# The second projection's buffers opened one tile sooner, and the last group's fourth product with its sums and splits pinned together, in an encoder layer on one core

## The chip, the core and the metric

The kernel runs on one core of a Trainium2 chip. The metric is the device time of one execution in microseconds (us). The unchanged kernel took 1143.36 us as the median of three runs (1142.58, 1143.36 and 1144.24).

## What is computed

One layer of an encoder over 1024 positions of width 1024: a norm, an input projection that feeds a pooling mixer and a chunked attention, an output projection, then a gated MLP, a per-layer gate and a last norm. The change touches only the MLP, here cut to its core:

```python
hn = rmsnorm(h, norm_ffn_g[i])
up = hn @ w_up[i]                                  # 1024 x 5632
gt, val = up[..., :D_FF], up[..., D_FF:]           # D_FF = 2816
gt = causal_dwconv(gt, conv_w[i], conv_b[i])
h = h + (jax.nn.gelu(gt, approximate=False) * val) @ w_down[i]
```

## The kernel before, in words

Every matrix product is float32. An operand is held as two parts, hi (the value rounded to the matmul type) and lo (the rest). Making the pair is a **split** (`split`, lines 132 to 137): ACT writes hi (L133), then DVE writes lo (L134). Where the operand is taken negative, the pair is L988 on ACT and L989 on DVE. `mm3` (lines 126 to 130) then issues three matmuls: hi by hi (L128), hi by lo (L129), lo by hi (L130).

The MLP's hidden width is cut into 22 tiles of 128 (`fi` from 0 to 21). For each, `up(fi, ...)` makes the gate and value rows of the tile. It uses a seven-product scheme for a two-by-two block product, so `steps` lists seven products, from `fi` = 2 on in the order 1, 5, 6, 2, 7, 3, 4. One product is 12 matmuls of 128x512. Their weights come from four quarters of `w_up`, loaded by SP into a ring of six raw buffers (`fetch`, L699). DVE adds quarters to each other where a product needs a sum (`summed`, L703), and the result is split into a ring of three (`prepare`). A raw buffer is loaded again once its last reader is done. The tile's activation is then formed on ACT and DVE: L811 and L812, the convolution L837 to L839, GELU L840, and L854/L856, or L847 in the last two tiles. For the first 20 tiles SP stores it to a scratch tensor `Yd` in DRAM (L898).

The **second projection** (by `w_down`) takes the 20 stored tiles in five groups of four (g from 0 to 4), again with seven products each, in the order 1, 2, 5, 4, 6, 7, 3. One is 24 matmuls (`down_next`), whose four results DVE adds into the residual (L1006). Both sides of a product (w: `w_down`; a: `Yd`) are loaded into the raw buffers `RW`, kinds "one" and "grow". The first source of a buffer is loaded by SP (L956) and further ones are added in flight by a DMA from POOL's queue (L954). `split_next` splits them into one set of pairs (`BQ` and a piece of `R`), so the splits for the next product must wait until PE has read the set for the last one. `ask` issues the loads whose buffers are free. In group 4, product 4, the a side is the sum of its "one" and "grow" buffers, added on DVE (L984, one for each of two buffers).

PE's order is written out by hand. The down products stand between up products: in the last two tiles, product (4, 5) follows product 3 of tile 20, and product (4, 4) follows product 1 of tile 21. The orders on DVE, ACT, SP and POOL are set when the program is built, by a scheduler that puts each instruction where its own model finds it ready. An instruction marked `keep_in_program_order` keeps its written place among the pinned ones, and `issue_after` keeps a load behind the one named. Each of these engines works strictly in its order.

`RW` and `BQ` are opened after tile 1 (L1018), in memory that an earlier buffer held, and the first loads stand behind tile 1's store. After tile 21 the tail begins, for which `late_pairs` loads and splits twelve pieces (two of `pT`, four of `w_ple`, four of `w_down`, two of `pT`; L1066) into raw buffers that the last `w_up` quarters leave.

Of the kernel before, what the change touches and what calls it, by code (L numbers as in the profile page):

```python
# [93 lines left out]
def trunk(tc, xT, pT, vecs, w_qk0, w_in, w_v, bias, counts, pool_w, w_out, w_up, w_down,  # L94
# [4 lines left out]
    with tc.tile_pool(name="sb", bufs=1) as sb, \  # L99
# [587 lines left out]
        prepared, fetched, done = [0], [0], [0]  # L687
        held = {}
        used = [False] * len(rawu)

        def fetch(upto):

            while fetched[0] < len(loads) and loads[fetched[0]][0] < upto and not used[fetched[0] % len(rawu)]:
                _, owner, (v, z) = loads[fetched[0]]
                i = fetched[0] % len(rawu)
                fetched[0] += 1
                used[i] = True
                fi = owner if isinstance(owner, int) else owner[0]
                sp.dma_start(rawu[i], w_up[fi, v, :, z * 512:(z + 1) * 512])  # L699
                held[owner, (v, z)] = i  # L700

        def summed(to, a, b, op=ALU.add):
            dve.tensor_tensor(rawu[to], rawu[a], rawu[b], op)  # L703

        def prepare(upto):
            while prepared[0] < min(upto, len(order)):
# [5 lines left out]
                if (fi, n) in alone:  # L712
                    t, = done_with = [held[(fi, n), q] for q in FORMS[n]]
                else:
                    a11, a12, a21, a22 = [held.get((fi, q)) for q in ((0, 0), (0, 1), (1, 0), (1, 1))]
                    if n == 5:
                        summed(a21, a21, a22)
                    elif n == 6:
                        summed(a21, a21, a11)
                    elif n == 3 and fi < 2:  # L720
                        summed(a11, a21, a12)
                    elif n == 7:
                        if fi > 1:
# [247 lines left out]
        def split_next(pinned=False):  # L971
# [3 lines left out]
            if not all((side, g, n) in asked for side in "wa"):  # L975
                return
            nsplit[0] += 1
            for side in "wa":
                sign = -1.0 if side == "a" and n in NEGATIVE else 1.0
                for j in range(2):  # L980
                    t = raws[side, buffer(side, n), j]
                    hi, lo = pairs[side, j]
                    if (side, g, n) == ("a", 4, 4):
                        tc.keep_in_program_order(dve.tensor_tensor(t, t, raws["a", "grow", j], ALU.add))  # L984
                    if sign > 0:
                        split(t, hi, lo, pinned)
                    else:
                        act.activation(hi, t, AF.Copy, scale=-1.0)  # L988
                        dve.scalar_tensor_tensor(lo, t, -1.0, rv(hi), ALU.mult, ALU.subtract)  # L989
                split_done.add((side, g, n))  # L990
            ask()

# [22 lines left out]

        for fi in range(4):
            up(fi, negative(fi))
            if fi == 1:  # L1018
                b_pool = tc.tile_pool(name="bq", bufs=1)
                bp = b_pool.__enter__()  # L1020
                B = bp.tile([P, 3072], F32R, name="BQ")
# [2 lines left out]
                for s, side in enumerate("wa"):  # L1024
                    for j in range(2):
                        p_ = spots[2 * s + j]
                        pairs[side, j] = p_[:, 0:512], p_[:, 512:1024]
                        for q, kind in enumerate(("one", "grow")):
                            z = 4 * s + 2 * q + j
                            raws[side, kind, j] = RW[:, 512 * z:512 * (z + 1)]  # L1030
                with tc.issue_after(written[0].ins):
                    ask()
            if fi == 2:
                for d in range(4):
# [26 lines left out]
        def late_pairs(n):  # L1061
            for _ in range(n):
                src, hi, lo = pieces[npiece[0]]
                t = late[npiece[0]]
                npiece[0] += 1
                sp.dma_start(t, src)  # L1066
                split(t, hi, lo, True)

        up(last_f[0], None, downs(last_f[0], (3, 5)))
# [217 lines left out]
```

## Time and profile before

| | |
|---|---|
| median of three runs | 1143.36 us |
| the profiled execution's own time | 1145.58 us |
| its span, first to last instruction | 1143.8 us |
| PE busy | 1129.3 us, 99% of the span |
| DVE busy | 890.4 us, 78% |
| ACT busy | 604.6 us, 53% |
| mean granted TensorE clock | 0.995 |

The profiled execution took 1.8 us more than its span, for what lies before the first and behind the last instruction. A matmul of 128x512 is shown as 0.39 us but they start about 0.227 us apart, since each overlaps the next. So a loss on PE is best seen where two starts lie further apart than that. In a row of the timeline, the bracket tells how long the engine was idle ahead of the instruction and what ended that. Several like instructions that follow each other share one row with their count.

### The profile page before, as it was taken

The numbers are of one execution on the slowest core, as the hardware profiler recorded it, in microseconds if no ns is written. First come the engines' busy times: TensorE is split into PE (matmuls) and PEld (weight loads), VectorE is DVE, ScalarE is ACT, GpSimd is POOL, SyncE is SP. The second block draws the span as 40 slices with busy tenths as digits, with TensorE's granted clock in tenths as the row PEclk, the third lists the DMA queues.
The fourth block names the chain that finished last, engine by engine and source line by source line (L and its number), as shares of the span: only waits on it lengthen the run. The fifth ranks groups of instructions, "written<-read, shape, count | busy, mean of one in ns | idle before, by whom it ended". The sixth has DMA issues, their size and how long they took to land.

```text
span 1143.8 us, 15743 instructions
## 1 busy us (share of the span) xinstructions
PE 1129.3 (99%) x5675; PEld 957.4 (84%) x5675; DVE 890.4 (78%) x1546; ACT 604.6 (53%) x1071; POOL 143.1 (13%) x188
## 2 busy tenths in 40 slices
PE   8999999999999999999999999999999999999997
PEld 7988998888888887888888888888888887888897
DVE  7678878879658887887788778877887787986864
ACT  8568677765645544434353435343534444564644
POOL 0000000073002200120112011201120112000000
PEclk9999999999999999999999999999999998999999
DMA  7110102114500146574557455745584556420012
GB/s 265 38 49 31 49 13 68 40 28 143 180 19 10 38 132 171 145 172 135 156 148 173 132 157 148 175 130 157 143 176 132 148 146 128 132 93 19 1 75 74
DMA packets 64446, 124.84 MB, mean 109 GB/s; under 512 B 7280, under 2 KB 8560, under 8 KB 64368
## 3 DMA queue, kind: packets, MB, share of 16 engines
q1 hardware_dynamic: 50400, 98.60, 26.0%
q0 software_dynamic: 13824, 25.17, 13.6%
q8 instruction: 44, 0.72, 0.3%
q14 instruction: 34, 0.28, 0.1%
q10 hardware_dynamic: 144, 0.07, 0.0%
HBM read 109.13 MB, written 14.68 MB: 108 GB/s over the span
## 4 chain that ended last, share of the span: by engine, by line
PE 87%; DVE 6%; issue 2%; ACT 2%; DMA 2%; POOL 1%; SPq 0%; DVEq 0%; POOLq 0%; ACTq 0%
PE PS L129 26%; PE PS L128 26%; PE PS L130 26%; PE PS L370 2%; DVE R L134 2%; PE PS L388 1%; PE PS L387 1%; PE PS L345 1%; PE PS L344 1%; DMA F<-in_w_up 1%; ACT R L133 1%; DMA F<-in_w_qk 1%; PE PS L353 0%; PE PS L352 0%; DVE F L703 0%
## 5 line engine op out<-in xcount | busy, mean ns | idle before, releaser
L128 PE MATMUL PS<-R 128*128 128x512 f32 (+1 forms) x1176 | 442.9, 377 | 2.7 <-ACT R L232 1.4
L130 PE MATMUL PS<-R 128*128 128x512 f32 (+1 forms) x1176 | 438.1, 373 | 0.0
L129 PE MATMUL PS<-R 128*128 128x512 f32 (+1 forms) x1112 | 420.1, 378 | 0.3 <-DVE R L233 0.3
L128 PEld LDWEIGHTS PS<-R 128*128 128x128 f32 x1176 | 221.7, 189 | 40.8 <-ACT R L232 1.8
L130 PEld LDWEIGHTS PS<-R 128*128 128x128 f32 x1176 | 221.5, 188 | 39.2 <-DVE R L134 0.4
L129 PEld LDWEIGHTS PS<-R 128*128 128x128 f32 x1112 | 209.7, 189 | 36.6 <-DVE R L233 0.6
L133 ACT ACTIVATE R<-F 128x512 fp32r<-128x512 f32 (+2 forms) x225 | 140.7, 637 | 178.7 <-PE PS L129 80.8
L134 DVE TENSOR_TENSOR R<-F,R 128x512 fp32r<-128x512 f32 (+2 forms) x221 | 152.7, 700 | 55.2 <-ACT R L133 54.3
L133 ACT ACTIVATE BQ<-RW 128x512 fp32r<-128x512 f32 x90 | 52.6, 622 | 88.6 <-PE PS L129 87.1
L1006 DVE TENSOR_TENSOR F<-F,PS 128x512 f32<-128x512 f32 x140 | 92.3, 682 | 7.4 <-PE PS L130 7.4
L703 DVE TENSOR_TENSOR F<-F 128x512 f32<-128x512 f32 x88 | 60.6, 688 | 41.0 <-DMA F<-in_w_up 39.2
L954 POOL DMA_DIRECT2D RW<-Yd x56 | 48.7, 870 | 241.1 <-DMA RW<-Yd 176.6
L954 POOL DMA_DIRECT2D RW<-in_w_down x40 | 35.7, 956 | 254.9 <-DMA RW<-in_w_down 223.0
L134 DVE TENSOR_TENSOR BQ<-RW,BQ 128x512 fp32r<-128x512 f32 x90 | 59.1, 686 | 2.5 <-PE PS L129 1.3
L128 PE MATMUL PS<-R,BQ 128*128 128x512 f32 x140 | 55.3, 395 | 1.1 <-ACT R L988 1.1
L129 PE MATMUL PS<-BQ 128*128 128x512 f32 x140 | 55.1, 394 | 0.6 <-DVE BQ L989 0.6
L356 ACT ACTIVATE F<-F,small 128x640 f32<-128x640 f32 (+2 forms) x64 | 44.4, 693 | 21.2 <-DVE small L354 13.1
L128 PE MATMUL PS<-BQ 128*128 128x512 f32 x140 | 55.1, 394 | 0.4 <-ACT BQ L988 0.4
L129 PE MATMUL PS<-R,BQ 128*128 128x512 f32 x140 | 55.2, 394 | 0.3 <-DVE R L989 0.3
L130 PE MATMUL PS<-R,BQ 128*128 128x512 f32 x140 | 55.0, 393 | 0.0
L130 PE MATMUL PS<-BQ 128*128 128x512 f32 x140 | 55.0, 393 | 0.0
L612 ACT ACTIVATE F<-F 128x512 f32<-128x512 f32 (+1 forms) x49 | 27.9, 570 | 45.5 <-DVE F L1154 16.7
(188 smaller groups left out, 1808.5 us busy)
## 6 DMA issues: line engine op xcount, KB each, us to landing
F<-in_w_up SPq DMA_DIRECT2D x91, 256.0 KB, 4.4
RW<-Yd SPq DMA_DIRECT2D x60, 256.0 KB, 3.7
RW<-Yd POOLq DMA_DIRECT2D x56, 256.0 KB, 4.9
RW<-in_w_down SPq DMA_DIRECT2D x50, 256.0 KB, 2.8
Yd<-F SPq DMA_DIRECT2D x40, 256.0 KB, 3.0
RW<-in_w_down POOLq DMA_DIRECT2D x40, 256.0 KB, 6.4
F<-in_w_in SPq DMA_DIRECT2D x10, 512.0 KB, 3.8
F<-in_xT SPq DMA_DIRECT2D x16, 256.0 KB, 5.8
```

The lines of the kernel that those rows point to most:

```text
L128: pe.matmul(ps, ahi, bhi, start=first, stop=False, skip_group_check=more)
L129: pe.matmul(ps, ahi, blo, start=False, stop=False, skip_group_check=more)
L130: pe.matmul(ps, alo, bhi, start=False, stop=last, skip_group_check=more)
L133: both = (act.activation(hi, src, AF.Copy), dve.tensor_tensor(lo, src, rv(hi), ALU.subtract))
L134: dve.tensor_tensor(lo, src, rv(hi), ALU.subtract))
L344: pe.matmul(PS[:, 4 + z, 0:320], q, K2[:, ks], start=True, stop=False)
L356: act.activation(S[:, 0:n], S[:, 0:n], AF.Exp, bias=s_[:, 0:1], scale=-1.0, accum_out=s_[:, 1:2])
L370: pe.transpose(pst[:, j * P:(j + 1) * P], S[:, j * P:(j + 1) * P], ident)
L612: act.activation(self.q, src, AF.Square)
L703: dve.tensor_tensor(rawu[to], rawu[a], rawu[b], op)
L954: pool.dma_start(t, src, accum_op=ALU.add)
L1006: dve.tensor_tensor(t, t, PS[:, 4 + d], ALU.subtract if n in (1, 5) else ALU.add)
```

## The change

Four things change. First, `RW` and `BQ` are opened after tile 0 and not after tile 1, and the first loads are held behind the latest `w_up` load instead of behind tile 1's store. Second, in the last tile the sum for product 5 (L703 with n = 5) is pinned. Third, for group 4's product 4, the two sums L984 come ahead of all its splits, and sums and splits are pinned. Fourth, the loads of `late_pairs` are held behind the latest `w_up` load.

```diff
@@ fetch
-                sp.dma_start(rawu[i], w_up[fi, v, :, z * 512:(z + 1) * 512])
+                newest[0] = sp.dma_start(rawu[i], w_up[fi, v, :, z * 512:(z + 1) * 512])
@@ prepare
                     if n == 5:
-                        summed(a21, a21, a22)
+                        s5 = summed(a21, a21, a22)
+                        if fi == NF - 1:
+                            tc.keep_in_program_order(s5)
@@ split_next
             nsplit[0] += 1
+            if (g, n) == (4, 4):
+                pinned = True
+                for j in range(2):
+                    t = raws["a", "one", j]
+                    tc.keep_in_program_order(dve.tensor_tensor(t, t, raws["a", "grow", j], ALU.add))
             for side in "wa":
                 sign = -1.0 if side == "a" and n in NEGATIVE else 1.0
                 for j in range(2):
                     t = raws[side, buffer(side, n), j]
                     hi, lo = pairs[side, j]
-                    if (side, g, n) == ("a", 4, 4):
-                        tc.keep_in_program_order(dve.tensor_tensor(t, t, raws["a", "grow", j], ALU.add))
                     if sign > 0:
                         split(t, hi, lo, pinned)
                     else:
                         act.activation(hi, t, AF.Copy, scale=-1.0)
-                        dve.scalar_tensor_tensor(lo, t, -1.0, rv(hi), ALU.mult, ALU.subtract)
+                        low = dve.scalar_tensor_tensor(lo, t, -1.0, rv(hi), ALU.mult, ALU.subtract)
+                        if pinned:
+                            tc.keep_in_program_order(low)
@@ the loop over the first four tiles
             up(fi, negative(fi))
-            if fi == 1:
+            if fi == 0:
                 b_pool = tc.tile_pool(name="bq", bufs=1)
...
-                with tc.issue_after(written[0].ins):
+                with tc.issue_after(newest[0].ins):
                     ask()
@@ late_pairs
-                sp.dma_start(t, src)
+                with tc.issue_after(newest[0].ins):
+                    sp.dma_start(t, src)
                 split(t, hi, lo, True)
```

The built programs have the same instructions; PE's order is the same throughout. Line numbers of the changed file are 2 to 8 higher (L956 is L958 there, L898 is L900, L1006 is L1013, L989 is L994; L703, L984 and L134 keep theirs).

**SP, start of the second projection.** This is SP's queue from the last loads of tile 0 on (`Yd_3418` and `Yd_3419` are the stores of tiles 0 and 1), before:

```order
L699 DMA F<-in_w_up 128x512 x9
L898 DMA Yd_3418<-F 128x512 x2
L699 DMA F<-in_w_up 128x512 x2
L898 DMA Yd_3419<-F 128x512
L956 DMA RW<-in_w_down 128x512
L898 DMA Yd_3419<-F 128x512
L956 DMA RW<-in_w_down 128x512 x3
L956 DMA RW<-Yd_3418 128x512
L956 DMA RW<-Yd_3419 128x512
L956 DMA RW<-Yd_3418 128x512
L956 DMA RW<-Yd_3419 128x512
L699 DMA F<-in_w_up 128x512 x4
```

The same stretch of SP's queue in the changed kernel:

```order
L699 DMA F<-in_w_up 128x512 x7
L958 DMA RW<-in_w_down 128x512 x4
L699 DMA F<-in_w_up 128x512 x2
L900 DMA Yd_3418<-F 128x512 x2
L699 DMA F<-in_w_up 128x512
L958 DMA RW<-Yd_3418 128x512 x2
L699 DMA F<-in_w_up 128x512
L900 DMA Yd_3419<-F 128x512 x2
L699 DMA F<-in_w_up 128x512
L958 DMA RW<-Yd_3419 128x512 x2
L699 DMA F<-in_w_up 128x512 x3
```

The four `w_down` loads and the two loads of tile 0's store moved ahead, among the `w_up` loads of tiles 1 to 3; the two loads of tile 1's store stay where the eight were. Among the last four `w_up` loads the order differs too: before, the first is the quarter that completes tile 3's product 5, then tile 3's (0, 1) quarter; in the changed kernel a quarter of tile 4 comes first, then tile 3's (0, 1), and the one that completes tile 3's product 5 is third.

**DVE, ahead of and at the product (4, 4).** DVE's order from the sum for tile 21's product 5 (the first row) to tile 20's L812, before:

```order
L703 TENSOR_TENSOR F<-F 128x512
L1006 TENSOR_TENSOR F<-F,PS 128x512 x3
L134 TENSOR_TENSOR BQ<-RW,BQ 128x512
L1006 TENSOR_TENSOR F<-F,PS 128x512
L134 TENSOR_TENSOR BQ<-RW,BQ 128x512 x2
L134 TENSOR_TENSOR R<-RW,R 128x512
L134 TENSOR_TENSOR R<-F,R 128x512
L819 TENSOR_TENSOR V<-PS,F 128x512
L845 TENSOR_TENSOR V<-V,F 128x512
L811 TENSOR_TENSOR F<-PS,F 128x512
L134 TENSOR_TENSOR R<-F,R 128x512
L812 TENSOR_TENSOR F<-F 128x512
```

And from there, in the changed kernel, starting at the three additions of the same product's results:

```order
L1013 TENSOR_TENSOR F<-F,PS 128x512 x3
L134 TENSOR_TENSOR BQ<-RW,BQ 128x512
L1013 TENSOR_TENSOR F<-F,PS 128x512
L134 TENSOR_TENSOR BQ<-RW,BQ 128x512 x2
L134 TENSOR_TENSOR R<-RW,R 128x512
L134 TENSOR_TENSOR R<-F,R 128x512
L821 TENSOR_TENSOR V<-PS,F 128x512
L703 TENSOR_TENSOR F<-F 128x512
L847 TENSOR_TENSOR V<-V,F 128x512
L813 TENSOR_TENSOR F<-PS,F 128x512
L134 TENSOR_TENSOR R<-F,R 128x512
L814 TENSOR_TENSOR F<-F 128x512
```

The L703 moved from ahead of the additions to behind L819 (L821 there). A little further on DVE prepares product (4, 4); from the last addition of (4, 5)'s results on, before:

```order
L1006 TENSOR_TENSOR F<-F,PS 128x512
L134 TENSOR_TENSOR BQ<-RW,BQ 128x512 x2
L134 TENSOR_TENSOR R<-F,R 128x512
L984 TENSOR_TENSOR RW<-RW 128x512
L822 TENSOR_TENSOR V<-PS,F 128x512
L703 TENSOR_TENSOR F<-F 128x512
L989 SCALAR_TENSOR_TENSOR BQ<-RW,BQ 128x512
L134 TENSOR_TENSOR R<-F,R 128x512
L984 TENSOR_TENSOR RW<-RW 128x512
L847 TENSOR_TENSOR F<-F,V 128x1024
L989 SCALAR_TENSOR_TENSOR R<-RW,R 128x512
L703 TENSOR_TENSOR F<-F 128x512
```

In the changed kernel the same stretch reads:

```order
L1013 TENSOR_TENSOR F<-F,PS 128x512
L984 TENSOR_TENSOR RW<-RW 128x512 x2
L134 TENSOR_TENSOR R<-F,R 128x512
L134 TENSOR_TENSOR BQ<-RW,BQ 128x512 x2
L994 SCALAR_TENSOR_TENSOR BQ<-RW,BQ 128x512
L994 SCALAR_TENSOR_TENSOR R<-RW,R 128x512
L134 TENSOR_TENSOR R<-F,R 128x512
L824 TENSOR_TENSOR V<-PS,F 128x512
```

Both sums now stand ahead of the splits, the two lo parts of the a side (L989, L994 there) follow each other, and the two sums L703 for tile 21's product 7 have gone out of the stretch, to behind the splits for product (4, 6).

**ACT, the same place.** ACT's order from the GELU's first step of tile 20 to product (4, 4)'s last split, before:

```order
L837 ACTIVATE F<-F,vec 128x1024
L133 ACTIVATE BQ<-RW 128x512 x2
L840 ACTIVATE F<-F 128x1024
L133 ACTIVATE R<-F 128x512
L988 ACTIVATE BQ<-RW 128x512
L133 ACTIVATE R<-F 128x512
L792 ACTIVATE PS<-PS 128x512
L988 ACTIVATE R<-RW 128x512
```

And in the changed kernel:

```order
L839 ACTIVATE F<-F,vec 128x1024
L842 ACTIVATE F<-F 128x1024
L133 ACTIVATE R<-F 128x512
L133 ACTIVATE BQ<-RW 128x512 x2
L993 ACTIVATE BQ<-RW 128x512
L993 ACTIVATE R<-RW 128x512
```

The two hi parts of the w side (L133) moved behind the GELU (L840, L842 there) and the split behind it, and the a side's two (L988, L993 there) now follow without a step between them.

**SP, the late pieces.** Near the end SP has four loads of `Yd` into `RW`, two for the product (4, 7) and two for (4, 3). The first `w_ple` load stood behind the first of these; in the changed kernel all four `w_ple` loads stand behind all four, the last two of which wait until the a side's splits for (4, 6) have been made.

More of the change, by code (lines that the diff above doesn't have):

```diff
@@ L686, in trunk @@
                 loads += [(i, fi, q) for q in need if not any(l[1] == fi and l[2] == q for l in loads)]
-        prepared, fetched, done = [0], [0], [0]
+        prepared, fetched, done, newest = [0], [0], [0], [None]
         held = {}
@@ L698, in fetch @@
                 fi = owner if isinstance(owner, int) else owner[0]
-                sp.dma_start(rawu[i], w_up[fi, v, :, z * 512:(z + 1) * 512])
+                newest[0] = sp.dma_start(rawu[i], w_up[fi, v, :, z * 512:(z + 1) * 512])
                 held[owner, (v, z)] = i
         def summed(to, a, b, op=ALU.add):
-            dve.tensor_tensor(rawu[to], rawu[a], rawu[b], op)
+            return dve.tensor_tensor(rawu[to], rawu[a], rawu[b], op)
         def prepare(upto):
```

## The prediction

> **What bounds the kernel now.** I read the page first, then PE's list of waits, then PE's own timeline at the places that the list names. The page says how much there is to win at all.
>
> ```profile
> span 1143.8 us, 15743 instructions
> PE 1129.3 (99%) x5675; PEld 957.4 (84%) x5675; DVE 890.4 (78%) x1546; ACT 604.6 (53%) x1071; POOL 143.1 (13%) x188
> ```
>
> PE is busy for 99% of the span. An edit that leaves PE's work and order as they are, as this one does, can only win where PE stands still or runs slowly. PE's list of waits is short:
>
> ```profile
> PE PS L128 <- ACT R L988: 1.1, 1, 1.1
> PE PS L128 <- ACT PS L792: 1.0, 1, 1.0
> ...
> PE PS L128 <- ACT R L133: 0.3, 1, 0.3
> ```
>
> L792 and one L133 belong to tile 3, near 442 us (place A). L988 belongs to product (4, 4), near 952 us (place B), where the list has three more rows of L988 and L989. Those are the two places that the change touches. PE's rows there, start and length:
>
> ```profile
> 438.73 0.39 PE L129 MATMUL PS<-R 128*128 128x512 f32 x1
> 441.00 0.39 PE L130 MATMUL PS<-R 128*128 128x512 f32 x1
> 442.35 0.50 PE L128 MATMUL PS<-R 128*128 128x512 f32 x1 [0.96 <-ACT PS L792]
> 448.38 0.50 PE L128 MATMUL PS<-R 128*128 128x512 f32 x1 [0.29 <-ACT R L133]
> 449.44 0.39 PE L128 MATMUL PS<-R 128*128 128x512 f32 x1
> ...
> 951.76 0.39 PE L130 MATMUL PS<-R 128*128 128x512 f32 x1
> ...
> 956.64 0.79 PE L129 MATMUL PS<-R,BQ 128*128 128x512 f32 x1 [0.28 <-DVE R L989]
> 962.11 0.40 PE L130 MATMUL PS<-R,BQ 128*128 128x512 f32 x1
> ```
>
> From 438.73 to 441.00 are 10 starts, so the undisturbed pace is 0.227 us. From 441.00 to 449.44 are 28 starts: they took 8.44 us and would take 6.36, so **A costs 2.1**. From 951.76 to 956.64 are 5 starts, 4.88 us for 1.14: 3.75 lost in waits. From there to 962.11 are 13 starts, 5.47 us for 2.95: 2.5 lost with nothing to wait for. The clock column (the one ahead of DMA share and GB/s) tells why:
>
> ```profile
> 445.00:450.00 5.00, 4.71 (x20) 3.29 (x19) 4.90 (x9) 2.41 (x5) 0.00 (x0) 1.00 0.60 208
> 955.00:960.00 5.00, 4.15 (x9) 2.97 (x10) 3.93 (x5) 1.57 (x2) 0.88 (x1) 0.50 0.90 185
> 960.00:965.00 5.00, 5.00 (x19) 4.01 (x19) 2.66 (x5) 1.95 (x4) 0.86 (x1) 0.82 0.93 199
> ```
>
> After the four waits of B the granted clock was halved for some 6 us; after those of A it stayed at 1.00. **B costs 6.3** with it. Together 8.4 us, 0.7% of the time, is the most that these places can give.
>
> **Place A, part by part.** Why was the seed L792 late? Back along its engines:
>
> ```profile
> 427.10 3.27 SPq L699 DMA_DIRECT2D F<-in_w_up  x4
> F<-in_w_up SPq DMA_DIRECT2D x7, 256.0 KB, 7.7
> 425.00:430.00 5.00, 5.00 (x24) 4.15 (x23) 1.98 (x3) 1.69 (x3) 1.97 (x2) 1.00 1.12 296
> 425.60 0.69 DVE L134 TENSOR_TENSOR R<-F,R 128x512 fp32r<-128x512 f32 x1 [0.94 <-ACT R L133]
> 434.83 0.69 DVE L703 TENSOR_TENSOR F<-F 128x512 f32<-128x512 f32 x1 [2.56 <-DMA F<-in_w_up]
> 437.97 1.25 ACT L837 ACTIVATE F<-F,vec 128x1024 f32<-128x1024 f32 x1 [1.69 <-DVE F L812]
> 441.72 0.57 ACT L792 ACTIVATE PS<-PS 128x512 f32<-128x512 f32 x1
> ```
>
> SP issued tile 3's quarter at 427.10, behind eight loads of the second projection. It took 7.7 us (median in this stretch), DVE stood for it until 434.83, and ACT, late by as much, went without a pause from L837 to L792. PE wanted L792 finished at 441.0 + 0.23.
>
> In the changed kernel six of the eight loads go 10 to 27 us sooner. The order shows that the wanted quarter does not go out much sooner itself: it is now third of the last four, and its buffer is free only when the L134 of 425.60 has ended, 426.29, so 0.8 sooner than 427.10. What changes is its company. In the 6.4 us before 427.10 SP issued two stores and eight loads, 2.6 MB at 256 KB each, 8.9 us of traffic at the 296 GB/s of that row; six of them, 5.3 us, are gone. 7.7 - 5.3 is 2.4. The page's median of all `w_up` loads (its row stands with rival 4) is 4.4 us, and I take that: landing near 430.7, with bounds of 428.7 (2.4) and 434.0 (7.7, no relief).
>
> Then the next thing that DVE waits for is PE: tile 2's product 3, whose last start is 12 x 0.227 x 3 before 441.00, 432.83, with its end near 433.3. L811, L134 and L812 at 0.60 each (this pace and ACT's 0.52 come out of rows of place B) end at 435.2; ACT's L837 (1.25) ends near 436.45, then come L133, three splits into `BQ`, the one into `R` that now precedes the seed, and one more L133, at 0.52 apart: L792 can start near 439.6 and is wanted by 440.6. So the stall goes, with 1 us to spare, as long as the quarter lands by 433.2. The L133 at 448.38 hangs on the same backlog of DVE and goes with it. At the late bound some 1.6 of the 2.1 would stay, and none at the early one. I take 0.1 left: **A gives 2.0.**
>
> The sooner loads cost nothing that I can find: memory and queue are free there, near 394 us, where this row has the DMA engines at a third.
>
> ```profile
> 390.00:400.00 10.00, 9.95 (x47) 7.90 (x46) 8.56 (x14) 5.60 (x9) 0.00 (x0) 1.00 0.33 105
> ```
>
> Without that cover, they would delay `w_up` loads by 0.9 us each, and those issued there are needed 10 us later or more. The two loads of tile 0's store wait for that store on SP, but the next `w_up` load stands behind them only from 408 to 410.4, when its own buffer comes free.
>
> **Place B.** DVE and ACT around it:
>
> ```profile
> 934.83 0.69 DVE L703 TENSOR_TENSOR F<-F 128x512 f32<-128x512 f32 x1 [3.11 <-DMA F<-in_w_up]
> 934.96 1.68 ACT L133 ACTIVATE BQ<-RW 128x512 fp32r<-128x512 f32 x3 [4.07 <-PE PS L129]
> 935.44 1.88 DVE L1006 TENSOR_TENSOR F<-F,PS 128x512 f32<-128x512 f32 x3
> 938.36 0.63 ACT L133 ACTIVATE R<-F 128x512 fp32r<-128x512 f32 x1 [1.20 <-PE PS L129]
> 940.24 0.68 DVE L134 TENSOR_TENSOR R<-F,R 128x512 fp32r<-128x512 f32 x1
> 948.75 0.68 DVE L1006 TENSOR_TENSOR F<-F,PS 128x512 f32<-128x512 f32 x1
> 951.16 0.68 DVE L984 TENSOR_TENSOR RW<-RW 128x512 f32<-128x512 f32 x1
> 954.16 0.69 DVE L984 TENSOR_TENSOR RW<-RW 128x512 f32<-128x512 f32 x1
> 955.90 0.68 DVE L989 SCALAR_TENSOR_TENSOR R<-RW,R 128x512 fp32r<-128x512 f32 x1
> ```
>
> Three in 1.68 on ACT are 0.63 + 2 x 0.52, three in 1.88 on DVE 0.68 + 2 x 0.60: so far apart do such instructions start. DVE stood 3.11 for the last quarter and then ran without a pause to 956.6. Pinning product 5's sum behind L819 takes this wait out: the three L1006 run as PE finishes their banks, and the first thing to hold DVE is the L133 that waits for PE until 938.36, so its L134 starts at 939.05 instead of 940.24. The moved L703 takes 0.60 of this back. Everything to the fourth L1006 stays in order, so that one starts near 948.1 instead of 948.75.
>
> Behind it come the sums at 948.7 and 949.3, ended at 950.0. ACT's GELU ends near 949.2; its L133 has to wait for PE's product 4 of tile 20, which ended at 949.2 too (12 starts ahead of 951.76, plus 0.39). At 0.52 each: L133 at 949.25, w at 949.8 and 950.3, the a side's two L988 at 950.8 and 951.3, ended at 951.4 and 951.95. PE arrives at 951.99 and finds its hi operands. DVE: L134 at 949.95, w's lo at 950.55 and 951.15, L989 at 951.75 and 952.35, ended at 952.4 and 953.0. PE wants the first at 952.22 and the second at 953.1: a wait of 0.25 is left and about 0.1 for starting again. The chain is tight at three points, each good to a few tenths: bounds are 0 and 1.5 left. I take 0.35: **B gives 5.9**, the halved clock included.
>
> What is late next? DVE loses the pauses that it had while PE stood, among them this one:
>
> ```profile
> 969.81 0.69 DVE L134 TENSOR_TENSOR R<-F,R 128x512 fp32r<-128x512 f32 x1 [2.03 <-ACT R L133]
> ```
>
> In new time that L134 is due at 963.5; by the same walk (15 instructions from 953 on, the two L703 included) DVE is there near 964.3, waiting for PE again within one product. The splits for (4, 6) need two additions from POOL, freed by the sums now near 949.5 instead of 952 and 955: earlier, and wanted at 963.4.
>
> **The sum.** 1145.58 - 2.0 - 5.9 = 1137.7 for a profiled execution. The median of the runs is 2.2 below the profiled one; carried over, 1135.5, and I say **1135.6**.
>
> **A rule against it.** The Trainium skill (TensorE: Matmul & The Clock Gate, Part 1) says that the gate judges PE by a window of about 3.4 us that runs freely, so that the place of a change of clock varies from run to run. The trace agrees that it needs a dense group of waits (B and not A); one execution cannot show how it varies.
>
> **The rivals.** (1) The clock did not fall in the timed runs; the profiled one's 2.2 more are the 2.5 of B. For: the sizes agree, and the runs spread by 1.7. Against: the waits of B are long and dense in any run. Then only waits are won: 1143.36 - 2.0 - 3.4 = 1138.0. (2) The quarter at A lands late (434.0): 1135.6 + 1.6 = 1137.2. Against: the traffic that delayed it has gone. (3) DVE becomes the bound behind 953 us. It is busy 9.79 of 10 us here:
>
> ```profile
> 980.00:990.00 10.00, 10.00 (x45) 8.28 (x45) 9.79 (x16) 5.39 (x10) 0.00 (x0) 1.00 0.38 132
> ```
>
> If it does not catch up near 964, B's gain is handed back and only A's stays: 1141.4. (4) The four `w_ple` loads, now behind SP's wait for (4, 6), land late; ACT and DVE take their splits in order, ahead of those for (4, 3). They go out near 962 to 967, right behind the `Yd` loads that (4, 6)'s splits free, and are wanted near 975, 5.9 ahead of these four splits of before:
>
> ```profile
> 981.27 2.18 ACT L133 ACTIVATE R<-F 128x512 fp32r<-128x512 f32 x4
> ```
>
> ```profile
> F<-in_w_ple SPq DMA_DIRECT2D x4, 256.0 KB, 6.5
> F<-in_w_up SPq DMA_DIRECT2D x91, 256.0 KB, 4.4
> ```
>
> So a landing up to 8 us is hidden, and 6.5 is the median. Each us beyond is PE's, plus 2.5 for the clock once PE stands long. From a landing of some 13.5 us on (5.5 + 2.5 = 8) it is slower than before; at 17 us, 1146.9. (5) The scheduler's order does not bring the operands sooner and the waits move: 1143.4.
>
> **How the numbers follow.** My forecast 0.50, (1) 0.25, (2) 0.08, (3) 0.06, (4) 0.06, (5) 0.05. A measurement of this kernel tells about 0.2%, 2.3 us, from no change. Forecast, (1) and (2) are faster: 0.83; (3) and (5) within: 0.11; (4) slower: 0.06. The range reaches from both stalls at nothing (0.45 less) and the runs' scatter of 0.8, 1134.3, to (1) with B's late bound, 1139.2.
>
> **What would show it.** Right: no wait of PE on L792 near 442, DVE's L703 there ahead of 433.2, the sums back to back near 949, PE at (4, 4) with a wait under 0.5 and a clock of 1.00 near 955. Wrong: a wait on L984, a new wait of PE between 960 and 1000, SP standing ahead of `w_ple` beyond 968, or a profiled execution that falls by 8 and a median that falls by 5.

## The result, and the profile after

The changed kernel takes **1137.3 us** as the median of six runs (1136.74 to 1137.53). The unchanged one beside it takes 1142.97 (1142.21 to 1144.24, six runs). The ratio is 0.9946, with a 95% interval of 0.9935 to 0.9956: it is faster by 5.7 us, 0.5%. The forecast was 1135.6, with a range of 1134.3 to 1139.2. The profiled execution took 1137.53 us, where the working had 1137.7. So the profile fell by 8.0 us, as forecast (7.9), and the median by 2.4 less than that.

PE's list of waits in the changed kernel is this, whole. L232 and L233 stand at the start of the program:

```profile
PE PS L216 <- DVE B L214: 1.5, 1, 1.5
PE PS L370 <- DVE B L378: 0.8, 2, 0.5
PE PS L129 <- DVE R L233: 0.3, 1, 0.3
PE PS L1228 <- ACT F L612: 0.3, 1, 0.3
PE PS L128 <- ACT R L232: 0.2, 1, 0.2
```

Nothing of tile 3 and nothing of product (4, 4) is left in it.

**Place A.** In this profile the matmul ahead of the one that waited starts 0.1 us sooner than in that of before (440.93 for 441.00). The rows are SP's, DVE's, ACT's (L794 is the former L792) and PE's:

```profile
424.38 0.80 SPq L958 DMA_DIRECT2D RW<-Yd  x2
425.27 4.13 SPq L699 DMA_DIRECT2D F<-in_w_up  x3
...
429.50 0.69 DVE L703 TENSOR_TENSOR F<-F 128x512 f32<-128x512 f32 x1 [0.45 <-DMA F<-in_w_up]
...
439.40 0.57 ACT L794 ACTIVATE PS<-PS 128x512 f32<-128x512 f32 x1
...
440.93 0.39 PE L130 MATMUL PS<-R 128*128 128x512 f32 x1
441.16 0.39 PE L128 MATMUL PS<-R 128*128 128x512 f32 x1
```

Only two loads of `Yd` stand ahead of the three quarters now. DVE has its quarter at 429.50, where before it was 434.83. The seed begins at 439.40 (forecast 439.6 in the time of before, so 439.5 here). The matmul that waited until 442.35 before now starts at 441.16, at PE's pace of 0.23, and the 28 starts that took 8.44 us take 6.35.

**Place B.** Here the profile runs 2.2 us ahead of that of before (951.76 has become 949.57). DVE, ACT and PE at product (4, 4):

```profile
946.43 1.29 DVE L984 TENSOR_TENSOR RW<-RW 128x512 f32<-128x512 f32 x2
948.69 0.62 ACT L993 ACTIVATE BQ<-RW 128x512 fp32r<-128x512 f32 x1
949.21 0.61 ACT L993 ACTIVATE R<-RW 128x512 fp32r<-128x512 f32 x1
949.57 0.39 PE L130 MATMUL PS<-R 128*128 128x512 f32 x1
949.58 0.69 DVE L994 SCALAR_TENSOR_TENSOR BQ<-RW,BQ 128x512 fp32r<-128x512 f32 x1
949.79 0.39 PE L128 MATMUL PS<-BQ 128*128 128x512 f32 x1
950.19 0.69 DVE L994 SCALAR_TENSOR_TENSOR R<-RW,R 128x512 fp32r<-128x512 f32 x1
950.33 0.50 PE L129 MATMUL PS<-BQ 128*128 128x512 f32 x1
```

The two sums are back to back. PE finds its first hi operand, and its one late start is at 950.33, 0.54 behind the last, so 0.3 lost, and 0.41 with the next start. The clock stays whole (again the column ahead of DMA share and GB/s; these rows hold all engines):

```profile
950.00:955.00 5.00, 4.86 (x21) 3.86 (x21) 4.87 (x8) 2.00 (x3) 0.07 (x1) 1.00 0.96 240
955.00:960.00 5.00, 5.00 (x24) 4.13 (x23) 4.97 (x9) 2.91 (x5) 3.27 (x4) 1.00 0.83 156
```

**The start.** A third difference between the two profiles has nothing to do with the change. It is the matmul that waits for L232, before and after:

```profile
10.12 0.49 PE L128 MATMUL PS<-R 128*128 128x512 f32 x1 [1.41 <-ACT R L232]
```

```profile
9.58 0.50 PE L128 MATMUL PS<-R 128*128 128x512 f32 x1 [0.16 <-ACT R L232]
```

It started 0.5 us sooner by chance: across the profiles below this wait lies between 0.4 and 2.0 us with no edit near it. By 441 us only 0.1 of the 0.5 is left. That 0.1, 2.1 between there and 951.76, and 5.9 behind it make up the 8.0.

### The profile page after: what moved, and what is told of

Its sections match the earlier page's. It is cut to its first block, busy times and chain, and to the rows that moved or that the text cites. A ratio compares the mean times of both kernels' runs of the same rounds, so it can differ in the third digit from the quotient of the medians.

```text
span 1135.8 us, 15750 instructions
## 1 busy us (share of the span) xinstructions
PE 1126.1 (99%) x5675; PEld 956.0 (84%) x5675; DVE 891.0 (78%) x1546; ACT 604.5 (53%) x1071; POOL 143.1 (13%) x188
## 4 chain that ended last, share of the span: by engine, by line
PE 92%; DVE 3%; issue 2%; ACT 1%; POOL 1%; DMA 0%; SPq 0%; POOLq 0%; DVEq 0%; ACTq 0%
PE PS L128 28%; PE PS L129 28%; PE PS L130 28%; PE PS L370 2%; PE PS L388 1%; PE PS L387 1%; DVE R L134 1%; PE PS L345 1%; PE PS L344 1%; ACT R L133 1%; DMA F<-in_w_qk 0%; PE PS L353 0%; PE PS L352 0%; POOL TB L778 0%; DVE F L760 0%
## 5 line engine op out<-in xcount | busy, mean ns | idle before, releaser
L133 ACT ACTIVATE R<-F 128x512 fp32r<-128x512 f32 (+2 forms) x225 | 140.6, 637 | 173.9 <-PE PS L129 75.2
L134 DVE TENSOR_TENSOR R<-F,R 128x512 fp32r<-128x512 f32 (+2 forms) x221 | 152.8, 701 | 48.3 <-ACT R L133 47.5
L1013 DVE TENSOR_TENSOR F<-F,PS 128x512 f32<-128x512 f32 x140 | 92.6, 682 | 5.8 <-PE PS L130 5.6
L133 ACT ACTIVATE BQ<-RW 128x512 fp32r<-128x512 f32 x90 | 52.6, 622 | 81.1 <-PE PS L129 77.1
L703 DVE TENSOR_TENSOR F<-F 128x512 f32<-128x512 f32 x88 | 60.7, 689 | 39.0 <-DMA F<-in_w_up 37.2
L956 POOL DMA_DIRECT2D RW<-Yd x56 | 49.0, 875 | 260.3 <-DMA RW<-Yd 201.4
L956 POOL DMA_DIRECT2D RW<-in_w_down x40 | 35.5, 941 | 233.5 <-DMA RW<-in_w_down 189.7
L134 DVE TENSOR_TENSOR BQ<-RW,BQ 128x512 fp32r<-128x512 f32 x90 | 59.2, 687 | 1.8 <-PE PS L129 1.3
L839 ACT ACTIVATE F<-F,vec 128x1024 f32<-128x1024 f32 (+1 forms) x25 | 28.6, 1143 | 44.2 <-DVE F L814 40.8
```

The costliest lines, as they stand in the source:

```text
L133: both = (act.activation(hi, src, AF.Copy), dve.tensor_tensor(lo, src, rv(hi), ALU.subtract))
L134: dve.tensor_tensor(lo, src, rv(hi), ALU.subtract))
L703: return dve.tensor_tensor(rawu[to], rawu[a], rawu[b], op)
L839: act.activation(y, Gb[:, 2 + a:2 + b], AF.Identity, bias=vec[:, C_CB + fi:C_CB + fi + 1], scale=cw(2))
L956: pool.dma_start(t, src, accum_op=ALU.add)
L1013: dve.tensor_tensor(t, t, PS[:, 4 + d], ALU.subtract if n in (1, 5) else ALU.add)
```

## The experiments

Each kernel was timed beside the unchanged one on the same chip; kernels with the same unchanged median beside them shared a chip. "Clock" counts the runs whose mean granted clock was 0.997 or less; an undisturbed run has 0.998 or 0.999.

| kernel | median us (runs) | unchanged beside it | ratio, 95% interval | clock 0.997 or less |
|---|---|---|---|---|
| unchanged again | 1143.80 (12) | 1144.17 | 1.0002, 0.9993 to 1.0011 | 11 of 12 |
| early opening alone | 1143.34 (11) | 1144.17 | 0.9994, 0.9985 to 1.0003 | 10 of 11 |
| all but the early opening | 1137.85 (5) | 1144.17 | 0.9945, 0.9932 to 0.9958 | 0 of 5 |
| all but the pin on product 5's sum | 1139.32 (7) | 1144.17 | 0.9963, 0.9950 to 0.9976 | 2 of 7 |
| changed again | 1137.80 (5) | 1144.12 | 0.9944, 0.9926 to 0.9962 | 1 of 5 |
| all but the early opening, again | 1138.26 (5) | 1144.12 | 0.9951, 0.9936 to 0.9967 | 0 of 5 |
| sums 2 steps later | 1141.02 (9) | 1144.12 | 0.9974, 0.9964 to 0.9985 | 5 of 9 |
| sums 4 steps later | 1143.91 (10) | 1144.12 | 0.9999, 0.9989 to 1.0009 | 10 of 10 |
| opened after tile 1, behind `w_up` | 1138.36 (6) | 1143.45 | 0.9957, 0.9942 to 0.9972 | 1 of 6 |
| all but the sums ahead | 1143.20 (12) | 1143.45 | 0.9991, 0.9980 to 1.0002 | 8 of 12 |
| sums ahead, splits not pinned | 1138.00 (6) | 1143.45 | 0.9954, 0.9939 to 0.9969 | 1 of 6 |
| late loads not held | 1137.63 (6) | 1143.45 | 0.9946, 0.9932 to 0.9960 | 0 of 6 |

### Does the clock fall in the typical run?

No edit: the unchanged kernel as a kernel of its own.

> The unchanged kernel once more, as a kernel of its own, so that the clock and the span of each of its runs are listed. What is tested is the 2.2 us by which the profiled execution lay above the median. Theory 1 (the clock): the halved clock behind (4, 4), 2.5 us, is missing in most runs. Then most runs list a mean clock of 0.997 to 0.999 with a time near 1142.5 to 1143.5, and only those of 0.995 to 0.996 are near 1145; a profile without the dip shows starts 0.227 us apart right behind the waits. Theory 2 (the start): the clock falls in every run (0.995 to 0.996 throughout), and the 2.2 us come from another place, such as the wait on L232 near the start, 1.4 us in the profile of before and 0.2 in that of the changed kernel. The waits at A (2.1) and B (3.75) are there in either case.

Eleven of twelve runs list a clock of 0.993 to 0.997, and so do 56 of the 61 runs of the unchanged kernel that stood beside the experiments. Of these 61, the 44 with 0.996 or less have a median of 1144.2, the 17 others one of 1142.8. So theory 1, that the halved clock belongs to the profiled run, falls. The start is not what made the profiled run slow either: its wait on L232 was 0.4 us here, and it was the slowest again, 1147.05. But A's waits were longer in it:

```profile
442.97 0.50 PE L128 MATMUL PS<-R 128*128 128x512 f32 x1 [1.41 <-ACT PS L792]
449.01 0.50 PE L128 MATMUL PS<-R 128*128 128x512 f32 x1 [0.26 <-ACT R L133]
```

That is 1.67 us idle, against 1.25 in the first profile.

### What is A worth?

Two kernels divide the change. The first has only the early opening:

```diff
-            if fi == 1:
+            if fi == 0:
                 b_pool = tc.tile_pool(name="bq", bufs=1)
...
-                with tc.issue_after(written[0].ins):
+                with tc.issue_after(newest[0].ins):
                     ask()
```

> Only the first part of the change: the second projection's buffers open after tile 0, their first loads behind the latest w_up load. All orders near the end are those of before. My theory: A's 2.0 us go and B stays whole, so 1143.0 - 2.0 = 1141.0. Rival (the parts work together, the sooner loads alone do nothing): 1143.0. Rival (the sooner loads cost something elsewhere, hidden by B's gain): above 1143.0. Its profile should show no wait on L792 and the waits on L988 and L989 as before.

The second is the changed kernel with these lines as before. It ran twice, the second time beside the changed kernel.

> The whole change but its first part: buffers and first loads after tile 1 as before; product 5's sum pinned, sums and splits of (4, 4) pinned together, late loads behind the last w_up load. If the typical run has no halved clock, B gives the waits alone, 3.75 - 0.41 = 3.3 us: 1143.0 - 3.3 = 1139.7. If the typical run has it, 5.8 us: 1137.2. A's wait on L792 (1.0 to 1.1) stays in its profile. Together with the run of the first part alone it should add up to the whole change (5.7).

> The changed kernel once more, beside the next one on the same chip. Theory 1 (A's wait is as long in the typical run as in the profiled one): this kernel is 1.9 to 2.1 us faster than the one that opens the buffers after tile 1. Theory 2 (the wait on the late quarter is mostly that of the profiled execution, which was the slowest of its kernel in nearly all cases so far): the two differ by 0.3 to 0.8. Its own profiled time should be within 0.5 of its median, since it has no wait left that hangs on a load but the one on L232.

> All of the change but the early opening, once more, beside the changed kernel on the same chip: it has no halved clock at B, so its runs scatter little and A's price can be read from the difference. Theory 1 (A costs the typical run 2.0 us): median 1139.3 if the changed kernel is at 1137.3. Theory 2 (in the typical run the late quarter lands some 1.5 us sooner than in the profiled one): 1137.6 to 1138.1, and the profiled execution alone about 1.5 to 2 us above its median, as it was in the first look (1139.68 against 1137.85).

In their profiles the parts do what the forecast said: the first has no wait on L792 and all those on L988 and L989; the second has lost these as the changed kernel has, with 0.4 us left, and kept A's. The times give A less. The early opening alone brings 0.8 us (the interval goes from 1.7 faster to 0.3 slower). Without it the change loses 0.46 on one chip, and 0.7 over both looks (median 1138.12 of ten runs against 1137.44 of the changed kernel's eleven, which were not all on the same chips). By the ratios, 0.9945 and 0.9951 without it against 0.9946 and 0.9944 with it, it is worth between nothing and 0.8. Theory 1, A at 2.0, is outside of all of these; theory 2's 0.3 to 0.8 holds the middle of them. A's wait also differs between profiles of the same lines. In the second look it was

```profile
441.50 0.50 PE L128 MATMUL PS<-R 128*128 128x512 f32 x1 [0.28 <-ACT PS L794]
447.54 0.50 PE L128 MATMUL PS<-R 128*128 128x512 f32 x1 [0.28 <-ACT R L133]
```

only 0.56 us idle, where before it was 1.25 and 1.67. The idle time tells less than PE lost, since it counts only from the end of the matmul before, which is shown 0.39 us or more behind its start, and the next start is late as well. By the starts of the same 28 matmuls, which take 6.35 us undisturbed:

| profile | the 28 starts, us | lost at A | this execution above its kernel's median |
|---|---|---|---|
| unchanged | 441.00 to 449.44 | 2.1 | 2.6 (2.2 above the first three runs) |
| unchanged again | 441.18 to 450.07 | 2.5 | 3.3 |
| all but the early opening | 440.51 to 448.65 | 1.8 | 1.8 |
| the same again | 440.83 to 448.60 | 1.4 | 0.7 |
| opened after tile 1, behind `w_up` (below) | 442.98 to 451.08 | 1.7 | 3.0 |
| changed | 440.93 to 447.28 | 0 | 0.2 |

All five profiles with the late opening lose something near the 2.1 that was priced, and all five executions lie above their medians. Of the nine profiles without this loss, six lie between 1.1 us below and 0.7 above; the other three are 1.9 to 3.1 above and lost the clock at the start, as did the fifth row. The profiled execution is the slowest of its kernel's runs in 8 of the 13 kernels timed from the result on. So it is not a typical one, and what the medians point to is a smaller A in the runs without a profile. Only profiled executions have rows, so this is argued and not shown. The second look's profile was expected 1.5 to 2 us above its median and came 0.7 above.

The expectation that the changed kernel's profiled run would lie within 0.5 of its median missed: 1140.28 against 1137.80. Its rows at the start tell why, PE's wait and then PE's stretch with its clock:

```profile
10.30 0.50 PE L128 MATMUL PS<-R 128*128 128x512 f32 x1 [1.75 <-ACT R L232]
```

```profile
10.00:15.00 5.00, 4.41 (x11) 0.66 1.02 370
```

PE stood 1.75 us for L232 and the clock fell behind it, 11 starts in 5 us. The same stretch has 0.66 to 0.73 in three more profiles (the early opening alone, the one without product 5's pin, the one opened after tile 1 behind `w_up`) and 1.00 in the rest. So a low clock in a run's list can have its place at the start as well as at (4, 4).

B then has nearly all of the gain: without the early opening the change is faster than the unchanged kernel beside it by 6.3 us (4.8 to 7.8) and by 5.9 (3.8 to 7.3). Expected was that the two parts add up to the whole: 0.8 and 6.3 make 7.1 where the whole gave 5.7 and 6.3, which the intervals allow.

### Is it the tile or the queue?

The buffers open after tile 1 again, but the first loads stay behind the latest `w_up` load:

```diff
-            if fi == 0:
+            if fi == 1:
                 b_pool = tc.tile_pool(name="bq", bufs=1)
```

> The changed kernel with its buffers opened after tile 1 as before, but the first loads held behind the latest w_up load instead of behind tile 1's store. Six of the eight loads then go after tile 0's store and two w_up loads (some 411 us) and not near 394, and the late w_up quarter stands in the same company as in the changed kernel. Theory 1 (A is a matter of what is queued ahead of that quarter; the tile that the buffers open in does not matter): no wait on L794 in the profile, and the time of the changed kernel, 1137.3 to 1137.8. Theory 2 (the sooner loads near 394 cost the typical run something, which hides part of A's 2.0): 1136 to 1137. Theory 3 (the loads must be early): 1138.1 or more, with the wait back.

1138.36, with the wait back in the profile: theory 3's numbers, though the ratio of 0.9957 (0.9942 to 0.9972) cannot be told from the changed kernel's 0.9946, and the wait is what decides. SP, DVE and PE there show why it is back, and it was not the loads' lateness as such:

```profile
422.79 1.52 SPq L900 DMA_DIRECT2D Yd<-F  x2
424.63 0.66 SPq L699 DMA_DIRECT2D F<-in_w_up  x1
428.33 0.80 SPq L958 DMA_DIRECT2D RW<-Yd  x2
429.22 2.23 SPq L699 DMA_DIRECT2D F<-in_w_up  x3
...
435.12 0.69 DVE L703 TENSOR_TENSOR F<-F 128x512 f32<-128x512 f32 x1 [4.02 <-DMA F<-in_w_up]
...
444.48 0.50 PE L128 MATMUL PS<-R 128*128 128x512 f32 x1 [1.11 <-ACT PS L794]
```

The six sooner loads had gone out by 415.7. But the two loads of tile 1's store stand on SP until that store has landed, and the wanted quarter stands behind them. The store took until 428.33 here, 5.5 us from its first issue; in the changed kernel the same loads went out at 424.38, 3.2 us behind. So the quarter has company of two kinds, traffic and a place in the queue. The second one is still there in the changed kernel.

### Which edits make B?

The pin on product 5's sum taken away:

```diff
-                        if fi == NF - 1:
-                            tc.keep_in_program_order(s5)
```

> The changed kernel without the pin on the sum for product 5 of the last tile, which then stands ahead of the three additions again and waits for the last w_up quarter. My theory: DVE's pause of about 3.1 us returns, the sums of (4, 4) come 1.2 - 0.6 = 0.6 us later or more, and PE waits at (4, 4) for some 1.0 us instead of 0.41: 1137.3 + 0.6 = 1137.9, at most 1138.5. Rival (the pin is what carries the gain of B): the waits of 3.3 us come back whole, 1140.6. Rival (the pin does nothing, the sums alone carry it): 1137.3.

1139.32, so about 1.9 us of the gain (2.0 by the ratios): more than the 0.6 of my theory, less than the rival's 3.3. In its profile PE waits 0.79 and 0.53 us at (4, 4) and loses 1.9 with the restarts, 1.5 more than the changed kernel. Its low clock (two of seven runs) stands at the start in the profile, not here.

The sums back among the splits and the splits of (4, 4) not pinned, the pin on product 5's sum kept:

```diff
-            if (g, n) == (4, 4):
-                pinned = True
-                for j in range(2):
-                    t = raws["a", "one", j]
-                    tc.keep_in_program_order(dve.tensor_tensor(t, t, raws["a", "grow", j], ALU.add))
...
                     hi, lo = pairs[side, j]
+                    if (side, g, n) == ("a", 4, 4):
+                        tc.keep_in_program_order(dve.tensor_tensor(t, t, raws["a", "grow", j], ALU.add))
...
-                        low = dve.scalar_tensor_tensor(lo, t, -1.0, rv(hi), ALU.mult, ALU.subtract)
-                        if pinned:
-                            tc.keep_in_program_order(low)
+                        dve.scalar_tensor_tensor(lo, t, -1.0, rv(hi), ALU.mult, ALU.subtract)
```

> The changed kernel with the two sums of (4, 4) back among its splits and the lo parts of its a side not pinned; product 5's sum is still pinned. My theory: DVE reaches product (4, 4) 0.6 us sooner than before, and the rest of the scattered sums stays: some 3.0 us of waits at (4, 4) in place of 3.75, with the halved clock in most runs: 1137.5 + 2.6 + 2 = 1142.1. Rival (without DVE's pause the sums come in time wherever they stand): 1137.5 to 1138.5.

1143.20, 1.1 above my theory, far from the rival's, and not to be told from the unchanged kernel beside it, though A's wait is gone. DVE (L986 are the sums) and PE in its profile:

```profile
948.90 0.68 DVE L986 TENSOR_TENSOR RW<-RW 128x512 f32<-128x512 f32 x1
952.26 0.69 DVE L986 TENSOR_TENSOR RW<-RW 128x512 f32<-128x512 f32 x1
...
952.40 0.50 PE L129 MATMUL PS<-BQ 128*128 128x512 f32 x1 [1.60 <-DVE BQ L991]
953.67 0.80 PE L128 MATMUL PS<-R,BQ 128*128 128x512 f32 x1 [0.53 <-ACT R L990]
954.75 0.80 PE L129 MATMUL PS<-R,BQ 128*128 128x512 f32 x1 [0.28 <-DVE R L991]
```

```profile
955.00:960.00 5.00, 5.00 (x12) 3.93 (x13) 2.72 (x4) 0.18 (x1) 0.00 (x0) 0.50 1.04 236
```

The second sum stands 3.4 us behind the first, PE waits three times, and from 953.5 on, behind the first of these waits, the clock is halved: in the row's 5 us, 12 starts where the changed kernel has 24. This kernel's runs also tell what the clock is worth, if nothing else divides them. Four of twelve kept it (0.999) and took 1140.1 to 1140.9, median 1140.5. The other eight (0.995 to 0.997) took 1141.4 to 1144.2, median 1143.8. The Trainium skill (TensorE: Matmul & The Clock Gate, Part 1) has the gate judge PE by a window that runs freely. One kernel whose runs fall into two groups 3.3 us apart is in line with that, and so are the stretches of 3.41 us in the last section.

The pins on the splits taken away, the sums ahead kept:

```diff
             if (g, n) == (4, 4):
-                pinned = True
                 for j in range(2):
```

> The changed kernel with the sums ahead of the splits, but the splits of (4, 4) not pinned. DVE's order is the same; ACT makes the w side's two hi parts ahead of tile 20's GELU and not behind it. My theory: the GELU waits for DVE anyway and the a side's hi parts follow the sums, so at most 0.2 us either way: 1137.3 to 1137.8. Rival (the pins carry the gain): 1139 or more, with a wait on the a side's hi parts.

1138.00, 0.2 above the bound of my theory, at a ratio of 0.9954, against 0.9944 and 0.9946 of the changed kernel: not to be told from it. The last part undone:

```diff
-                with tc.issue_after(newest[0].ins):
-                    sp.dma_start(t, src)
+                sp.dma_start(t, src)
```

> The changed kernel without its fourth part: the late pieces' loads are not held behind the latest w_up load. One thing moves, on SP: a w_up load of the last tiles goes out one place later, behind a late piece's load, which puts it some 1 us later at most. My theory: DVE no longer waits for that quarter, so nothing: 1137.3 to 1137.8. Rival (that quarter is the one that completes the last tile's product 5, and its sum comes late with it): 1138.3 or more, DVE idle ahead of L703 near 938.

1137.63 at 0.9946, the changed kernel's own ratio. Neither of these edits is worth anything that can be measured.

### How much lateness brings the clock down?

Pinned steps on DVE ahead of the sums, two in the first kernel and four in the second:

```diff
             if (g, n) == (4, 4):
                 pinned = True
+                for kind, j in (("one", 1), ("grow", 1)):
+                    t = raws["a", kind, j]
+                    tc.keep_in_program_order(dve.tensor_tensor(t, t, t, ALU.max))
```

> The changed kernel with two pinned steps on DVE ahead of the two sums of (4, 4), each a maximum of a buffer with itself, so the sums are about 1.2 us later and nothing in the result changes. My theory (PE at (4, 4) hangs on DVE alone): PE waits there 0.41 + 1.2 = 1.6 us, the clock stays at 1.00 since the waits are few: 1137.3 + 1.2 = 1138.5. Rival (any wait here over 1 us brings the halved clock with it): 1138.5 + 2.5 = 1141.

> The same with four such steps; two others of DVE have moved ahead of the sums with them, so these are about 3.6 us later than in the changed kernel. My theory: PE waits 0.41 + 3.6 = 4.0 us at (4, 4), about what it did before the change (3.75), and then the clock is halved as before for some 5 us: 1137.3 + 3.6 + 2.5 = 1143.4, mean clock 0.995 or 0.996 in most runs. Rival (the clock falls because of other work near the end, not because of the waits): 1140.9 with a clock of 0.998.

With two, a split (L134) went ahead of the sums as well, so they came some 1.9 us later and not 1.2. PE waits once at (4, 4):

```profile
953.20 0.50 PE L129 MATMUL PS<-BQ 128*128 128x512 f32 x1 [1.85 <-DVE BQ L997]
```

Its median is 1141.02, above my 1138.5 and at the rival's 1141, though the rival's halved clock is in only five of nine runs. The runs divide: four keep the clock, with a median of 1140.1, and five do not, with a median of 1141.4. With four, PE waits twice, the clock falls in its profile, and all ten runs list 0.997 or less:

```profile
952.30 0.49 PE L128 MATMUL PS<-BQ 128*128 128x512 f32 x1 [2.53 <-ACT BQ L996]
954.05 0.50 PE L129 MATMUL PS<-BQ 128*128 128x512 f32 x1 [1.25 <-DVE BQ L997]
```

```profile
955.00:960.00 5.00, 5.00 (x17) 0.66 0.91 231
```

1143.91 against 1144.12 of the unchanged kernel: 3.8 us of waits at this place, put in by nothing but later sums and the splits behind them, give the whole gain back. That is the forecast's mechanism of B run backwards, and it excludes the rival that the clock falls because of other work near the end.

## Why the prediction was right, and where it was off

**Place A, the mechanism: right.** The quarter's company went, DVE had it 5 us sooner, L794 began within 0.1 us of the walk, and both waits are gone from the profile, worth 2.1 there where 2.0 was forecast.

**Place B: right, in its steps and in its size.** In the time of the new profile the walk had the sums at 946.5, the a side's hi parts at 948.6 and 949.1, its lo parts at 949.6 and 950.2, and 0.35 us left. The rows say 946.43, 948.69 and 949.21, 949.58 and 950.19, and 0.41. The kernels without the early opening gain 5.9 and 6.3 where the term was 5.9, the clock included. One reading was off: the clock did not fall after the four waits but within the third, at 954.97, and stayed down for 6.8 us, not some 6; the size of the term does not hang on it.

**The sum: right for the profiled execution, wrong for the median.** The step that failed is "the median of the runs is 2.2 below the profiled one; carried over". It was not an offset of every profile: in the changed kernel the two differ by 0.2, and with four steps more on DVE the profile lies 1.1 below. In the changed kernel's second look they differ by 2.5, from the start of the program. The mis-sized term is A: 2.1 us in the profile that I priced it from, 0.5 to 0.7 by the medians. So, by this working, 1.4 of the 2.2 stood in a term that the change removes, and could not be carried over as well. With 0.6 in place of 2.0 the sum is 1143.36 - 0.6 - 5.9 = 1136.9, and 1137.3 was measured. The prediction had named a profiled execution that falls by 8 and a median that falls by 5 as a sign of being wrong; they fell by 8.0 and 5.7. Nor is the range's holding 1137.3 all its own merit, since its upper end was set by rival 1. The rest lies within what the unchanged kernel's own median moves (1142.97 to 1144.17 between groups of runs).

**Rival 1, the likeliest after the forecast, came nearer to the measured time (1138.0) than the forecast (1135.6), for a wrong reason.** It had the halved clock in the profiled execution alone. The clock falls in nine runs of ten; by the medians it was A that was larger there.

**Rival 2, the late quarter.** Its price, 1.6 of A's 2.1, was not paid in the profile, but the kernel opened after tile 1 shows a way to it that I had not named: the store's landing, two places ahead in SP's queue.

**Rival 3** did not come: DVE is ahead again at 965.41, where it waits for PE, and PE's list has no wait there. **Rival 4** did not come either, by less than I gave it. The last `w_ple` loads, the page's row for all four, and ACT's four splits:

```profile
964.01 0.93 SPq L1074 DMA_DIRECT2D F<-in_w_ple  x2
...
973.27 2.18 ACT L133 ACTIVATE R<-F 128x512 fp32r<-128x512 f32 x4
```

```profile
F<-in_w_ple SPq DMA_DIRECT2D x4, 256.0 KB, 7.9
```

The landing took 7.9 us as the median, not 6.5; the last, issued near 964.6, took 8.2 and landed at 972.8, 0.5 us ahead of the splits. I had put the bound of what is hidden at 8. **Rival 5** is excluded by the order on DVE.

**What stays open:** why A costs the median run so much less than all five profiles with the late opening show. Only profiled executions have rows. That the quarter lands sooner in other runs of the unchanged kernel, or that the changed one still loses at A in some, are both argued and not shown. For the first speaks the kernel without the early opening, in its first look: all runs but its profiled one took 1137.5 to 1137.9, little more than the changed kernel's (in its second look they took 1138.1 to 1138.7). Against the second speaks that none of the nine profiles with the early opening loses anything at A.

## What to carry to other kernels

Price a wait from the profile, but ask on what it hangs. The waits that hang on an engine's order (B's) came to 3.7, 3.7 and 4.1 us in three profiles with the old order; the loss that hangs on when a load lands was 1.4 to 2.5 us in five profiles, and yet the medians gave it 0.8 at most. Several profiles that agree are still no estimate of the median where the profiled executions are the slow ones. When a profiled execution lies 2 us above its median, look for the 2 us among the waits that you are about to remove before you carry them over. And take an edit apart once it has paid: here two of the edits (the sums ahead and the pin on product 5's sum) make nearly all of the gain, one makes some half a microsecond, and two nothing that can be told.

## What the runs showed of the hardware

The granted clock does not fall at a fixed amount of waiting. By what PE lost at (4, 4) in a kernel's profile, the runs with a mean clock of 0.997 or less were: 0.4 us lost, 3 of 39 runs (two of the three are profiled, and fell at the start); 1.9 us, 2 of 7 (the profiled one fell at the start); 2.2 us, 5 of 9; 3.5 us, 8 of 12; 3.7 us, the unchanged kernel, 56 of 61; 4.3 us, 10 of 10. Where in a run without a profile the clock fell is not on record. The idleness need not be in one piece: in the kernel of 8 in 12 the longest wait is 1.60 us, in the unchanged one 1.14.

The traces tell more than I read from them at first: the clock changes only at the edges of stretches of 3.41 us. In the trace of before it is full for 948.90 us (278 x 3.413), halved for 6.83 (2), full for 177.49 (52); in all fourteen traces the times between two changes are such multiples, until the last fall, which the end of the program cuts short. These are the last stretch ahead of the fall and the first halved one, before; the first number behind the comma is PE's busy time:

```profile
951.56:954.97 3.41, 1.82 (x6) 0.65 (x4) 3.41 (x7) 1.72 (x4) 2.67 (x3) 1.00 0.69 177
954.97:958.39 3.42, 2.54 (x5) 1.75 (x6) 3.42 (x5) 1.60 (x2) 0.88 (x1) 0.50 0.82 152
```

PE had idled 1.59 of the 3.41 us, in two waits and a part of the third, when the clock fell. Ahead of all nine falls other than the one at the end of each program, five at (4, 4) and four near the start, it had idled 1.6 to 2.3 us in the stretch just ended. Behind stretches with 1.4 us or less the clock never fell (A's waits put up to 1.41 us into one); one with 1.92 us, in the kernel with four steps more, did not bring it down either, but the next one did. The kernel with two steps more shows how the same wait can pass. Its 1.85 us lie across an edge, and each of the two stretches keeps the clock:

```profile
949.31:952.72 3.41, 2.04 (x9) 1.28 (x7) 3.41 (x7) 2.83 (x6) 1.75 (x2) 1.00 0.18 18
952.72:956.13 3.41, 2.93 (x13) 2.44 (x14) 3.41 (x6) 0.02 (x1) 0.00 (x0) 1.00 0.86 156
```

Where the edges lie differs between executions: the full clock is first granted at 6.07 us in one profile of the unchanged kernel and at 7.60 in the other. That this is why runs of one kernel divide is read from the traces; no run tests it. The Trainium skill (TensorE: Matmul & The Clock Gate, Part 1) has the fall come after at least one idle window of about 3.4 us; the runs here say that less is enough, 1.6 to 2.3 us of idleness within such a stretch.

When the clock has fallen, starts are 0.427 us apart and not 0.227, for one stretch (six of the nine falls) or two (the other three, in which PE had idled 0.4 to 0.9 us in the first). By these numbers I estimate the loss at 3.41 x (1 - 0.227 / 0.427) = 1.6 us for one and 3.2 for two. So a stall of some 2 us is a lottery, and its second loss (1.4 to 3.3 us between the two groups of one kernel's runs) can be larger than the first.
